# The second mixing layer's end in two token halves, with the fetching tokens' searches beside the second half

## The chip, the cores and the metric

The kernel runs as one program on one NeuronCore of a Trainium2 chip. The metric is device time in microseconds (us) of one execution; lower is better. The core has five engines that run side by side: TensorE (PE, matmuls; its weight loads are listed apart as PEld), VectorE (DVE), ScalarE (ACT), GpSimd (POOL, here almost only issuing indirect DMAs) and SyncE (SP, here issuing weight loads). Sixteen DMA engines move data between HBM and the on-chip memory (SBUF).

## The reference

Two transformer blocks over 512 tokens of width 1024, all in float32. The first block (a gated linear attention beside a latent attention, then a mixture of 64 experts) is not touched. What follows is the second block's end, cut to what matters:

```python
# mixing layer: y_a (recurrence) and y_b (convolution) are 512 wide, gates 2 x 1024
g_a, g_b = split(sigmoid(gates), 2)            # gates = h @ w_in[:, ...]
merged = g_a * (y_a @ w_branch_hg) + g_b * (y_b @ w_branch_conv)
x = x + merged @ w_out
# retrieval layer over 16384 single-neuron experts
hf = rmsnorm(x, norm_ffn_g)
q = (hf @ w_query).reshape(t, 8, 2, 128)        # 8 heads, two halves
s1, s2 = q[:, :, 0] . keys1, q[:, :, 1] . keys2 # 128 scores each
v1, i1 = top_k(s1, 16); v2, i2 = top_k(s2, 16)
top_s, top_pos = top_k(v1[:, None] + v2[None], 16)
idx = (i1 * 128 + i2)[top_pos]; gate = softmax(top_s)
act = gelu(expert_u[idx] . hf)                  # 8*16 rows per token
x = x + sum(gate * act * expert_v[idx])
out = rmsnorm(x, norm_final_g)
```

## The kernel before

The four phases are functions: `phase_a` (first mixing layer), `phase_b` (the expert layer), `phase_c` (second mixing layer), `phase_d` (retrieval layer and output). Activations are kept feature by token: `hx` is 128 partitions x 8 blocks x 512 tokens. Instructions are not written in their final order: a planner simulates the program's timeline and gives each engine a fixed queue, taking at each moment the ready instruction of the best priority, which by default is the order of writing. A tile belongs to a pool and a tag with a number of buffers; an instruction that needs a buffer waits until an earlier tile has been released, and a pool that is opened where a closed one lay waits, tile by tile, for what lay there. The retrieval layer's last loop fixes PE's order by hand (`manual_schedule`).

**Weights.** `k.load` (L1541) brings a 1 MB piece on SP's queue into a ring of 4 buffers. `phase_c` adds a second ring of 2 for its whole length, so six pieces can be there. `split` (L59 on ACT, L60 on DVE) turns a piece of weights into a high and a low part with two buffers for each; `mm3` (L71) multiplies with three matmuls per 128 rows.

**End of `phase_c`.** For eight output blocks `u`, two `unit`s (gates `ga`, `gb`: 24 matmuls each) are followed, one block behind, by two `branch`es (`wa`, `wb`: 12 matmuls each), all 512 tokens wide; then eight blocks of `w2_out` (24 matmuls) are added to `hx` (L1103), squared (L1105) and summed by a 128x32 matmul (L502). Then come the norm's factors (L1108 to L529).

**`phase_d`.** Tokens 0 to 255 (the fetching tokens) get their experts' rows by indirect DMA; tokens 256 to 511 are computed densely against all 16384 experts in 128 chunks. In order of writing:

- norm of both halves into new tiles (L1161), `hx` written to DRAM as `hdr` and freed;
- `first(h, 0)` for eight heads: query matmuls (L1198), a copy, key matmuls (L1205), and `best`: the 16 best of 128 (L1178 to L1190); `rows_of` turns the fetching tokens to rows;
- `second(0)`, `second(1)`: the 16 best of the sums, their gates and expert numbers (to L1269). After that `gathered_u` can run: 256 gathers of 128 rows of `peer_u` (L1346 on POOL, 0.5 MB each), each dotted with its tokens on DVE (L1355). Six row buffers; 206 gathers are written before the dense loop ends, the others in the last loop;
- 128 chunks `u_chunk` (L1328: 8 matmuls of 256 tokens, each as two instructions, and a Gelu). The first `JR` = 68 results stay in SBUF (`ge`), the next `JP` = 60 go to DRAM (`st`). Beside the first 68 run `first(h, 1)` and `second(2)`, `second(3)`; beside the other 60 run 64 `gates` steps, one per chunk, which build the dense gates of four tokens on DVE (L1299, L1304, L1315), ACT (L1306, L1311) and PE (L1309);
- the last loop: 64 pairs of chunks of `peer_v` (L1495), with gathered rows of `peer_v` (L1346, L1384: four per pair) and the last 50 `peer_u` gathers between them. `residual` (L1337, L1339) adds `hdr` back through one buffer `hr`. Row buffers: 6 in `sb` and 6 in `lp`.

The pool `ep` holds the tiles of searches and gates; `lp` (with `hr`, `z` and rows) is opened in its place after it closes.

Of the kernel before, what the change touches and what calls it, by code (L numbers as in the profile page):

```python
# [511 lines left out]
def group_cols(k, s, out):  # L512

    for j in range(T // 128):
        k.nc.tensor.matmul(out[:, j:j + 1], s[:, 128 * j:128 * j + 128], k.pick, start=True, stop=True)
# [18 lines left out]
def col_rows(k, p, y):  # L534

    for j in range(T // 128):
        k.nc.tensor.matmul(p[:, 128 * j:128 * j + 128], y[:, j:j + 1].to_broadcast([128, 128]), k.ident,
                           start=True, stop=True)
# [270 lines left out]
def phase_c(k):  # L809
# [5 lines left out]
    with ExitStack() as ctx:  # L815
        sb = ctx.enter_context(tc.tile_pool(name="c_sb", bufs=1, reuse_waits="tile"))
        wk = ctx.enter_context(tc.tile_pool(name="c_wk", bufs=2, reuse_waits="tile"))
        ps = ctx.enter_context(tc.tile_pool(name="c_ps", bufs=1, reuse_waits="tile", space=PS))
        k.ring2 = (ctx.enter_context(tc.tile_pool(name="c_ring", bufs=2, reuse_waits="tile")), 2)
        hg = ctx.enter_context(ExitStack())  # L820
        hp = hg.enter_context(tc.tile_pool(name="c_hg", bufs=2, reuse_waits="tile"))
# [4 lines left out]
        def tmp(name, shape=(128, T), dt=FT):  # L826
            return wk.tile(list(shape), dt, name=name, tag="t", bufs=7)
# [38 lines left out]
        lm = sb.tile([128, 1 + len(LEVELS), 64], I8, name="lm")  # L866
# [3 lines left out]
        rmask = sb.tile([128, T], FT, name="rmask")  # L870
# [15 lines left out]
        def unit(name, i):  # L886
# [8 lines left out]
            p = pm()  # L895
            mm3(k, [(p, slice(0, T))], wh, wl, xh, xl)
# [161 lines left out]
        hg.close()  # L1058


        mp = ctx.enter_context(tc.tile_pool(name="c_mp", bufs=1, reuse_waits="tile"))
        ah, al, bh, bl = (mp.tile([128, 4, T], FR, name=n) for n in ("ah", "al", "bh", "bl"))
        m = mp.tile([128, 8, T], FT, name="m")
        for y, h, l in ((ya, ah, al), (yb, bh, bl)):
            for i in range(4):
                act(h[:, i], y[:, i], AF.Copy)
                tt(l[:, i], y[:, i], h[:, i].bitcast(FT), op=OP.subtract)

        def branch(name, u, h, l):
# [4 lines left out]
            p = pm("h", 4)  # L1074
            mm3(k, [(p, slice(0, T))], wh, wl, h, l)
            return p

        gates = []
        for u in range(8 + 1):
            if u < 8:  # L1080
                gates.append([tmp("ga"), tmp("gb")])
                for t, n in zip(gates[u], ("ga", "gb")):
                    tt(t, unit(n, u), r12[:, 0], op=OP.mult)
                    act(t, t, AF.Sigmoid)
            if u >= 1:
                v = u - 1
                ga, gb = gates[v]
                tt(m[:, v], branch("wa", v, ah, al), ga, op=OP.mult)
                tt(gb, branch("wb", v, bh, bl), gb, op=OP.mult)
                tt(m[:, v], m[:, v], gb, op=OP.add)  # L1090
        mh, ml = [sb.tile([128, 8, T], FR, name=f"m{i}", tag="big", bufs=2) for i in range(2)]
        for u in range(8):
            act(mh[:, u], m[:, u], AF.Copy)
            tt(ml[:, u], m[:, u], mh[:, u].bitcast(FT), op=OP.subtract)
        sums = pm("h")
        for u in range(8):
            if u % 2 == 0:
                w = k.load(I["w2_out"][u // 2], [128, 8, 256])
            o = 128 * (u % 2)
            wh, wl = split(k, wk, w[:, :, o:o + 128], [128, 8, 128], "w8", 2)  # L1100
            p = pm()
            mm3(k, [(p, slice(0, T))], wh, wl, mh, ml)
            tt(hx[:, u], hx[:, u], p, op=OP.add)  # L1103
            sq = tmp("sq")
            act(sq, hx[:, u], AF.Square)  # L1105
            group_sums(k, sums, u, sq)
        sq = tmp("sums")
        nc.vector.tensor_copy(sq, sums)  # L1108
        pt = pm("h")
        group_cols(k, sq, pt)  # L1110
        ts(k.rcol[:, 0], pt[:, 0:4], 1.0 / D, EPS, op0=OP.mult, op1=OP.add)
        k.rstd = col_rsqrt(k, sb, k.rcol[:, 0], "rd", k.rcol[:, 1])
    k.ring2 = (None, 0)


def phase_d(k):
# [10 lines left out]
    JR, JP = 68, 60  # L1127
# [3 lines left out]
    with ExitStack() as ctx:  # L1131
        dr = ctx.enter_context(tc.tile_pool(name="d_dram", bufs=1, space=bass.MemoryType.DRAM))
        sb = ctx.enter_context(tc.tile_pool(name="d_sb", bufs=1, reuse_waits="tile"))
        pg = ctx.enter_context(tc.tile_pool(name="d_pg", bufs=2, reuse_waits="tile", space=PS))
# [16 lines left out]
        rstd = pm("g", 2)  # L1151
        col_rows(k, rstd, k.rstd)

        xs = [ep.tile([128, 4, N0], FT, name="xs", tag="kept", bufs=3) for _ in range(2)]
        x = sb.tile([128, 8, ND], FT, name="x")
        ht = [sb.tile([128, D], FT, name=f"ht{j}") for j in range(NS)]
        for s in range(2):
            o = slice(N0 * s, N0 + ND * s)
            for c in range(8):
                y = x[:, c] if s else xs[c // 4][:, c % 4]  # L1160
                stt(y, hx[:, c, o], gain("norm_ffn_g_2", c), rstd[:, o], op0=OP.mult, op1=OP.mult)  # L1161

        hdr = dr.tile([128, 8, T], FT, name="hdr")
        nc.scalar.dma_start(hdr, hx)
        k.free_h()
        keys = ep.tile([128, 2048], FT, name="keys", tag="big").rearrange("p (a b) -> p a b", a=16)
        nc.scalar.dma_start(keys, I["peer_keys"])

        def rows_of(j):
            for c4 in range(2):  # L1170
                p = pm("o", 3)
                for c in range(4):
                    nc.tensor.transpose(p[:, 128 * c:128 * c + 128], xs[c4][:, c, 128 * j:128 * j + 128], k.ident)
# [18 lines left out]
        def first(h, s):  # L1192

            w = k.load(I["peer_wq"][h], [128, 8, 256])
            for side in range(2):
                p = pm()
                for c in range(8):
                    nc.tensor.matmul(p[:, 0:256], w[:, c, 128 * side:128 * side + 128],  # L1198
                                     x[:, c] if s else xs[c // 4][:, c % 4], start=c == 0, stop=c == 7)
                q = ep.tile([128, 256], FT, name="q", bufs=3)  # L1200
                act(q, p[:, 0:256], AF.Copy)
                p = pm("o", 3)
                for j in range(2):
                    o = slice(128 * j, 128 * j + 128)
                    nc.tensor.matmul(p[:, o], q[:, o], keys[:, 2 * h + side], start=True, stop=True)  # L1205
                best(side, h, 2 * s, p)

        ia = [sb.tile([128, 128], I32, name=f"ia{j}") for j in range(NS)]
        iat = [sb.tile([128, 128], I32, name=f"iat{j}") for j in range(NS)]
        gg = [sb.tile([128, 128], FT, name=f"gg{j}") for j in range(NS)]  # L1210
# [199 lines left out]
        for h in range(8):  # L1410
            first(h, 0)
            if h < NS:
                rows_of(h)
# [258 lines left out]
```

## Time and profile before

| what | us |
|---|---|
| median of 3 runs (lowest, highest) | 3018.57 (3017.64, 3019.36) |
| the profiled execution | 3018.37 |
| its span, first to last instruction | 3016.6 |

| engine | busy us | share of the span |
|---|---|---|
| PE | 2713.6 | 90% |
| PEld | 1594.1 | 53% |
| DVE | 1224.5 | 41% |
| ACT | 623.2 | 21% |
| POOL | 591.7 | 20% |

The mean granted PE clock is 0.958 of 2.4 GHz. The DMAs moved 912.93 MB, a mean of 303 GB/s. The shares are means over stages that have different limits, so stretches of the span are read one by one: a row of a stretch gives its length, each engine's busy time with the number of its instructions, the granted clock, the mean busy share of the DMA engines and their GB/s. In a timeline a row is a run of like instructions: start, length, engine, line, operation, output and inputs, shape, count, and in brackets the idle time before it with what ended it. Durations of neighbouring instructions overlap, so the pace is read from the distance of starts.

### The profile page before, as it was taken

What the parts mean: (1) busy time and instruction counts of PE and PEld (TensorE: products, weight loads), DVE (VectorE), ACT (ScalarE), POOL (GpSimd) and SP (SyncE); (2) the same over time, 40 slices, a digit from 0 to 9 for tenths busy, and PEclk for the clock granted to TensorE, in tenths of its full rate; (3) what the DMA queues carried; (4) which work ended last, traced back from release to release, by engine and by line L of the source; (5) the groups of instructions that cost most, each with busy time, mean ns of one, the idle gap of its engine ahead of it and who ended that gap; (6) DMA issues with size and microseconds to landing.
All of it is one profiled execution on the core that took longest, in us unless ns stands there. A gap on an engine that the chain in (4) does not pass through costs nothing. (4 is left out here: it accounts for less than half of the span.)

```text
span 3016.6 us, 35266 instructions
## 1 busy us (share of the span) xinstructions
PE 2713.6 (90%) x13794; PEld 1594.1 (53%) x13794; DVE 1224.5 (41%) x3040; ACT 623.2 (21%) x1304; POOL 591.7 (20%) x600
## 2 busy tenths in 40 slices
PE   8999888887888777699999997999998499999997
PEld 6877422322232222377777786888887333333332
DVE  5444411111111111268855389985888522200001
ACT  4333200000000000265333121122555300000000
POOL 1000100000000000000000005454433256544442
PEclk9979999999999999899999998999999699999999
DMA  4104899999999999912113239999999699999996
GB/s 158 42 1 154 367 421 421 421 421 421 420 421 420 421 421 376 376 60 85 56 56 112 92 132 355 365 381 361 379 363 350 225 399 412 412 410 363 401 401 252
DMA packets 185453, 912.93 MB, mean 303 GB/s; under 512 B 18864, under 2 KB 38464, under 8 KB 112192
## 3 DMA queue, kind: packets, MB, share of 16 engines
q1 hardware_dynamic: 83664, 602.85, 49.7%
q0 software_dynamic: 73728, 268.47, 23.0%
q10 hardware_dynamic: 27888, 39.29, 3.6%
q8 instruction: 110, 1.80, 0.2%
q14 instruction: 63, 0.52, 0.0%
HBM read 890.61 MB, written 19.92 MB: 302 GB/s over the span
## 5 line engine op out<-in xcount | busy, mean ns | idle before, releaser
L1328 PE MATMUL pa<-x,w 128*128 128x256 f32 x2048 | 455.4, 381 | 0.0
L1328 PEld LDWEIGHTS pa<-x,w 128*128 128x128 f32 x2048 | 385.9, 191 | 50.6
L1355 DVE SCALAR_TENSOR_TENSOR rows<-rows,ht 128x1024 f32<-128x1024 f32 x256 | 310.5, 1218 | 237.5 <-DMA rows<-in_peer_u_rows,ia 211.4
L1346 POOL DMA_INDIRECT rows<-in_peer_u_rows,ia x256 | 287.8, 1124 | 440.1 <-DVE rows L1355 211.1
L1346 POOL DMA_INDIRECT rows<-in_peer_v,iat x256 | 253.0, 988 | 292.1 <-PE os L1384 151.1
L712 PE MATMUL pr<-w,xs 128*32 128x512 f32 x1024 | 212.4, 697 | 91.6 <-DMA w<-in_expert_up 91.4
L732 PE MATMUL px<-w,ht 128*32 128x512 f32 x1024 | 223.2, 599 | 44.9 <-DMA w<-in_expert_down 35.5
L1495 PE MATMUL o<-w,ge 128*128 128x512 f32 x544 | 243.4, 600 | 0.0
L1495 PE MATMUL o<-w,gl 128*128 128x512 f32 x480 | 215.5, 602 | 4.4 <-DVE gl L1481 4.4
L71 PE MATMUL pm<-xg,w8h 128*128 128x512 f32 x640 | 206.4, 402 | 3.5 <-ACT cc L942 1.4
L712 PE MATMUL pg<-w,xs 128*32 128x512 f32 x1024 | 178.7, 612 | 19.3 <-DMA w<-in_expert_gate 19.3
L960 POOL MEMSET acc<- 128x1024 f32 x1 | 1.0, 952 | 936.4 <-PE px L732 936.4
L712 PEld LDWEIGHTS pr<-w,xs 128*32 128x32 f32 x1024 | 46.0, 124 | 245.1 <-DMA w<-in_expert_up 168.7
L1495 PEld LDWEIGHTS o<-w,ge 128*128 128x128 f32 x544 | 100.8, 191 | 139.4 <-issue 139.4
L732 PEld LDWEIGHTS px<-w,ht 128*32 128x32 f32 x1024 | 53.4, 109 | 203.0 <-DMA w<-in_expert_down 95.8
L718 DVE SCALAR_TENSOR_TENSOR hd<-pr,ga,hd 128x512 f32<-128x512 f32 x16 | 12.0, 751 | 361.6 <-PE pr L712 361.6
L1495 PEld LDWEIGHTS o<-w,gl 128*128 128x128 f32 x480 | 89.4, 191 | 131.0 <-issue 122.9
L1384 PE MATMUL os<-rows,z 128*32 128x512 f32 x1024 | 144.6, 600 | 5.4 <-DMA rows<-in_peer_v,iat 4.3
L1481 DVE TENSOR_TENSOR gl<-gl,g 128x256 f32<-128x256 f32 x60 | 21.5, 420 | 305.2 <-DMA gl<-st 305.2
L71 PEld LDWEIGHTS pm<-xg,w8h 128*128 128x128 f32 x640 | 120.8, 190 | 33.7 <-ACT w8h L59 2.0
L745 DVE TENSOR_TENSOR hT<-hT,po 128x512 f32<-128x512 f32 x128 | 86.0, 687 | 128.7 <-PE po L744 127.3
L59 ACT ACTIVATE w8h<-w 128x1024 fp32r<-128x1024 f32 (+3 forms) x101 | 90.8, 901 | 218.7 <-PE pm L71 106.3
(561 smaller groups left out, 3601.8 us busy)
## 6 DMA issues: line engine op xcount, KB each, us to landing
w<-in_expert_up SPq DMA_DIRECT2D x128, 1024.0 KB, 19.8
w<-in_expert_gate SPq DMA_DIRECT2D x128, 1024.0 KB, 19.8
w<-in_expert_down SPq DMA_DIRECT2D x128, 1024.0 KB, 19.8
w<-in_peer_u SPq DMA_DIRECT2D x64, 1024.0 KB, 8.1
w<-in_peer_v SPq DMA_DIRECT2D x64, 1024.0 KB, 8.3
w<-in_peer_wq SPq DMA_DIRECT2D x16, 1024.0 KB, 4.8
w<-in_w_out SPq DMA_DIRECT2D x8, 1024.0 KB, 4.8
st<-kept ACTq DMA_DIRECT2D x15, 512.0 KB, 9.3
```

The lines of the kernel that those rows point to most:

```text
L59: nc.scalar.activation(hi, src, AF.Copy)
L71: nc.tensor.matmul(o, w[:, c, :], x[:, c, s], start=first and c == 0 and n == 0, stop=last and c == kc - 1 and n == 2)
L712: nc.tensor.matmul(p[s], xs[:, 4 * half + c, s], ws[e][:, c], start=half == 0 and c == 0, stop=half == 1 and c == 3, skip_group_check=True)
L718: stt(hd, pu, ga[:, 1:2], hd, op0=OP.mult, op1=OP.mult)
L732: nc.tensor.matmul(pd[n][s], ht[:, 2 * half + f, s], ws[e][:, f, 512 * n:512 * n + 512], start=half == 0 and f == 0, stop=half == 1 and f ...
L745: tt(hx[:, c], hx[:, c], p, op=OP.add)
L1328: nc.tensor.matmul(p[:, :ND], w[:, c], x[:, c], start=c == 0, stop=c == 7)
L1346: nc.gpsimd.indirect_dma_start(out=r, out_offset=None, in_=rows, in_offset=bass.IndirectOffsetOnAxis(ap=idx, axis=0))
L1355: stt(r, r, 1.0, ht[j], op0=OP.mult, op1=OP.mult, accum_out=dots[:, n:n + 1])
L1384: nc.tensor.matmul(po[i][32 * g:32 * g + 32], z[:, o:o + 32], rs[g][:, 512 * i:512 * i + 512], start=r == 0, stop=r == 31, skip_group_chec ...
L1481: tt(b, b, g[:, :, j], op=OP.mult)
L1495: nc.tensor.matmul(out[NS + t][c], w[:, 128 * t:128 * t + 128], vp[:, i % 2, 512 * c:512 * c + 512], start=i == 0, stop=i == NJ - 1, skip_ ...
```

## The change

The end of `phase_c` runs the whole chain (gates, branches, out, sums, norm factors) for tokens 0 to 255 and then again for 256 to 511, with matmuls 256 wide; each half loads and splits all weights. The second ring is closed with the recurrence's pools, so the ring has four buffers there. Halves of `hdr` are written as they are done, and the norm is made in place in `hx`, which now lives until the searches and dense chunks are done. Norm, `first`, `rows_of` and `second` of the fetching tokens are given the priority of the second half's beginning, and use the two PSUM banks "g"; scores lie in the same bank as their query. `JR` and `JP` become 64 and 64. Pools are laid out anew: `ge` at the bottom of phase C's place, then `lo` (gates' tiles, 3 row buffers; usable after the second half), `sb` (3 row buffers) and `ep` above; later `lp` with 3. Keys are loaded head by head, for each half.

```diff
@@ phase_c
+        hg = ctx.enter_context(ExitStack())
+        k.ring2 = (hg.enter_context(tc.tile_pool(name="c_ring", bufs=2, ...)), 2)
...
         hg.close()
+        k.ring2 = (None, 0)
+        HT = T // 2
+        mp = ctx.enter_context(tc.tile_pool(name="c_mp", bufs=1, reuse_waits="tile"))
+        pt6 = ctx.enter_context(tc.tile_pool(name="c_pt", bufs=1, ..., space=PS))
+        def pm(tag="m"):
+            return pt6.tile([128, 512], FT, ..., bufs={"m": 3, "h": 2, "s": 1}[tag])
...
+        for s in range(2):
+            S = slice(HT * s, HT * s + HT)
+            if s:
+                k.second_half = tc.cur_priority
+            yh, yl = (mp.tile([128, 8, HT], FR, name=f"y{i}", tag=f"y{i}") for i in range(2))
...
+                    for t, n in zip(gates[u], ("ga", "gb")):
+                        tt(t, unit(n, u, S, pm), r12[:, 0, S], op=OP.mult)
+                        act(t, t, AF.Sigmoid)
...
+            mh, ml = [mp.tile([128, 8, HT], FR, name=f"m{i}", tag=f"y{i}") for i in range(2)]
...
+                mm3(k, [(p, slice(0, HT))], wh, wl, mh, ml)
+                tt(hx[:, u, S], hx[:, u, S], p, op=OP.add)
+                sq = tmp("sq")
+                act(sq, hx[:, u, S], AF.Square)
+                group_sums(k, sums, u, sq)
+            nc.scalar.dma_start(k.hdr[:, :, S], hx[:, :, S])
...
@@ phase_d
-    JR, JP = 68, 60
+    JR, JP = 64, 64
...
+        ge = [gp.tile([128, n, ND], FT, name=f"ge{i}") for i, n in enumerate((JA, JR - JA))]
+        lo = ctx.enter_context(tc.tile_pool(name="d_lo", bufs=1, reuse_waits="tile"))
         sb = ctx.enter_context(tc.tile_pool(name="d_sb", bufs=1, reuse_waits="tile"))
...
+        x = [hx[:, :, 0:N0], hx[:, :, N0:]]
+        def norm(s):
+            rstd = pm("g", 2)
+            col_rows(k, rstd, k.rcol[:, 1, 2 * s:2 * s + 2], 2)
             for c in range(8):
+                stt(x[s][:, c], x[s][:, c], gain("norm_ffn_g_2", c), rstd[:, 0:256], ...)
...
-                p = pm()
+                p = pm() if s else pm("g", 2)
...
-                p = pm("o", 3)
+                r = p[:, 256:512]
...
-        rp.append((sb, 6))
+        rp.append((sb, 3))
+        with tc.high_priority(offset=tc.cur_priority - k.second_half):
+            norm(0)
+            for h in range(8):
+                first(h, 0)
+                if h < NS:
+                    rows_of(h)
+            for j in range(NS):
+                for _ in second(j):
+                    pass
+                pull(ga, 3)
+        norm(1)
+        rp.append((lo, 3))
...
         early.close()
+        k.free_h()
...
-        rp.append((lp, 6))
+        rp.append((lp, 3))
...
-            y = sb.tile([128, D], FT, name="rows", bufs=6)
+            y = sb.tile([128, D], FT, name="rows", bufs=3)
```

## Rows read from the trace of the kernel before

**Rows 1.** Stretches: length, busy us (instructions) of PE, PEld, DVE, ACT, POOL, clock, DMA

```profile
1500.00:1698.00 198.00, 193.09 (x802) 147.88 (x800) 90.07 (x120) 59.98 (x83) 2.16 (x2) 0.97 0.21 75
1698.00:1809.00 111.00, 107.78 (x528) 94.73 (x529) 83.47 (x464) 25.28 (x41) 0.00 (x0) 0.97 0.41 143
1809.00:1831.00 22.00, 1.40 (x8) 0.92 (x7) 18.70 (x38) 1.29 (x3) 16.60 (x13) 0.64 0.84 312
1831.00:2097.00 266.00, 265.95 (x1258) 234.33 (x1258) 217.80 (x701) 47.98 (x106) 131.86 (x116) 0.99 0.97 376
2097.00:2328.00 231.00, 230.26 (x1348) 200.77 (x1345) 194.50 (x440) 128.15 (x403) 85.11 (x74) 1.00 0.94 356
2328.00:2401.00 73.00, 23.50 (x150) 18.89 (x150) 48.45 (x116) 30.41 (x95) 24.09 (x19) 0.56 0.71 240
2401.00:2680.00 279.00, 274.11 (x914) 99.08 (x914) 59.52 (x97) 0.71 (x2) 161.09 (x159) 1.00 1.01 401
2680.00:2982.00 302.00, 301.31 (x1097) 114.85 (x1095) 17.21 (x48) 1.67 (x4) 125.64 (x133) 1.00 1.02 393
```

**Rows 2.** Timeline of PE, end of the first idle stretch

```profile
1830.45 0.47 PE L1269 MATMUL po<-cst,nn 128*128 128x128 f32 x1 [20.60 <-DVE nn L1267]
```

**Rows 3.** Timeline of PE, from the last dense chunk to the last loop

```profile
2324.74 1.94 PE L1495 MATMUL o<-w,ge 128*128 128x512 f32 x4
...
2385.31 3.62 PE L1339 MATMUL o<-cst,hr 128*128 128x128 f32 x16 [10.71 <-DMA hr<-hdr]
...
2397.12 3.78 PE L1339 MATMUL o<-cst,hr 128*128 128x128 f32 x16 [6.47 <-DMA hr<-hdr]
2400.69 4.39 PE L1495 MATMUL o<-w,ge 128*128 128x512 f32 x8
```

**Rows 4.** Stretch of the gates steps, columns as in rows 1

```profile
2097.00:2376.00 279.00, 244.53 (x1460) 211.74 (x1457) 238.93 (x545) 158.55 (x497) 104.53 (x89) 0.92 0.88 328
```

**Rows 5.** Timeline of PE, 512 columns wide, and the sums between two blocks

```profile
1660.34 0.40 PE L71 MATMUL pm<-m,w8l 128*128 128x512 f32 x1
...
1661.04 0.40 PE L71 MATMUL pm<-m,w8l 128*128 128x512 f32 x1
...
1662.54 1.04 PE L502 MATMUL ph<-sq,cst 128*32 128x512 f32 x2
1663.52 0.51 PE L71 MATMUL pm<-m,w8l 128*128 128x512 f32 x1
```

**Rows 6.** Timeline of PE in phase A: the same three matmuls, 264 columns

```profile
25.65 0.65 PE L71 MATMUL uu<-xg,w8h 128*128 128x264 f32 x4
...
26.38 0.64 PE L71 MATMUL uu<-xg,w8h 128*128 128x264 f32 x4
```

**Rows 7.** Groups by line: busy us, mean ns, idle us before and releasers

```profile
L60 DVE TENSOR_TENSOR w8l<-w,w8h 128x1024 fp32r<-128x1024 f32 x71 | 87.6, 1235 | 35.6 <-ACT w8h L59 34.9
L59 ACT ACTIVATE w8h<-w 128x1024 fp32r<-128x1024 f32 x71 | 74.9, 1056 | 140.1 <-PE pm L71 52.7 <-PE uu L71 23.4 <-issue 17.8
L1355 DVE SCALAR_TENSOR_TENSOR rows<-rows,ht 128x1024 f32<-128x1024 f32 x256 | 310.5, 1218 | 237.5 <-DMA rows<-in_peer_u_rows,ia 211.4 <-issue 16.9 <-PE o L1495 7.7
```

**Rows 8.** DMA issues: count, size, median us from issue to landing

```profile
w<-in_w_ga SPq DMA_DIRECT2D x4, 1024.0 KB, 4.8
```

**Rows 9.** Timeline of DVE: last addition, norm, two searches, first sums

```profile
1696.87 0.69 DVE L1103 TENSOR_TENSOR hT<-hT,pm 128x512 f32<-128x512 f32 x1 [4.93 <-PE pm L71]
...
1704.83 3.22 DVE L1161 SCALAR_TENSOR_TENSOR xs<-hT,vecs,pg 128x256 f32<-128x256 f32 x8 [2.23 <-PE pg L537]
...
1771.77 0.30 DVE L1178 MAX8 tv<-po 128x8 f32<-128x128 f32 x1 [0.95 <-PE po L1205]
...
1775.67 0.30 DVE L1178 MAX8 tv<-po 128x8 f32<-128x128 f32 x1 [0.94 <-PE po L1205]
...
1776.75 0.54 DVE L1221 TENSOR_TENSOR cand<-tv,tv 128x384 f32<-128x384 f32 x1
```

**Rows 10.** Timeline of POOL: the first gather

```profile
1809.27 1.16 POOL L1346 DMA_INDIRECT rows<-in_peer_u_rows,ia  x1 [124.51 <-DVE sm L1234]
```

More of the change, by code (lines that the diff above doesn't have):

```diff
@@ L509, in col_sums, with group_cols @@
             k.nc.tensor.matmul(out[:, j:j + 1], x[:, t0:t0 + 128], k.ones[:, 0:1], start=c == 0, stop=c == len(xs) - 1)
-def group_cols(k, s, out):
-    for j in range(T // 128):
+def group_cols(k, s, out, n=T // 128):
+    for j in range(n):
         k.nc.tensor.matmul(out[:, j:j + 1], s[:, 128 * j:128 * j + 128], k.pick, start=True, stop=True)
@@ L531, in col_rsqrt, with col_rows @@
     return out
-def col_rows(k, p, y):
-    for j in range(T // 128):
+def col_rows(k, p, y, n=T // 128):
+    for j in range(n):
         k.nc.tensor.matmul(p[:, 128 * j:128 * j + 128], y[:, j:j + 1].to_broadcast([128, 128]), k.ident,
@@ L1058, in phase_c, with tmp @@
         hg.close()
+        k.ring2 = (None, 0)
+        HT = T // 2
         mp = ctx.enter_context(tc.tile_pool(name="c_mp", bufs=1, reuse_waits="tile"))
[L1062 to L1067, printed above, removed]
+        pt6 = ctx.enter_context(tc.tile_pool(name="c_pt", bufs=1, reuse_waits="tile", space=PS))
+        def pm(tag="m"):
+            return pt6.tile([128, 512], FT, name="p" + tag, tag=tag, bufs={"m": 3, "h": 2, "s": 1}[tag])
+        def tmp(name):
+            return mp.tile([128, HT], FT, name=name, tag="t", bufs=6)
         def branch(name, u, h, l):
@@ L1091, in phase_c @@
[L1091 to L1106, printed above, removed]
@@ L1194, in first @@
             w = k.load(I["peer_wq"][h], [128, 8, 256])
+            keys = ep.tile([128, 2, 128], FT, name="keys", bufs=2)
+            nc.scalar.dma_start(keys, I["peer_keys"][:, 2 * h:2 * h + 2])
             for side in range(2):
[L1196 removed]
+                p = pm() if s else pm("g", 2)
                 for c in range(8):
[L1198 to L1200 removed]
+                    nc.tensor.matmul(p[:, 0:256], w[:, c, 128 * side:128 * side + 128], x[s][:, c],
+                                     start=c == 0, stop=c == 7)
+                q = ep.tile([128, 256], FT, name="q", bufs=2)
                 act(q, p[:, 0:256], AF.Copy)
[L1202 removed]
+                r = p[:, 256:512]
                 for j in range(2):
                     o = slice(128 * j, 128 * j + 128)
[L1205 to L1210, printed above, removed]
[L1211 to L1212 removed]
+                    nc.tensor.matmul(r[:, o], q[:, o], keys[:, side], start=True, stop=True)
+                best(side, h, 2 * s, r)
+        hk = lo.tile([128, 2, ND], F16, name="hk")
+        hg = lo.tile([128, 2, ND], FT, name="hg")
         def second(j):
@@ L1296, in gates @@
                     p = pm("g", 2)
-                    o1, o2, oh, ol = (ep.tile(sh, F16, name=f"o{n}", bufs=2) for n in range(4))
+                    o1, o2, oh, ol = (lo.tile(sh, F16, name=f"o{n}", bufs=2) for n in range(4))
                     for n, o in enumerate((o1, o2)):
@@ L1327, in u_chunk @@
             for c in range(8):
-                nc.tensor.matmul(p[:, :ND], w[:, c], x[:, c], start=c == 0, stop=c == 7)
+                nc.tensor.matmul(p[:, :ND], w[:, c], x[1][:, c], start=c == 0, stop=c == 7)
             act(dst, p[:, :ND], AF.Gelu)
@@ L1408, in routing @@
                 yield from second(j)
[L1410 to L1413, printed above, removed]
-        rp.append((sb, 6))
-        gp = ctx.enter_context(tc.tile_pool(name="d_ge", bufs=1, reuse_waits="tile", side="right"))
-        ge = [gp.tile([128, n, ND], FT, name=f"ge{i}") for i, n in enumerate((JA, JR - JA))]
-        rt, ga = routing(), chain(*(gathered_u(j) for j in range(NS)))
-        for j in range(NS):
-            for _ in second(j):
-                pass
-            pull(ga, 3)
-        taken = [0]
-        def some(n):
-            taken[0] += n
-            pull(ga, n)
+        rt, ga = routing(), chain(*(gathered_u(j) for j in range(NS)))
+        rp.append((sb, 3))
[11 more added lines that the diff above has]
+        rp.append((lo, 3))
         st = dr.tile([128, JP, ND], FT, name="st")
@@ L1558, in body @@
     nc.gpsimd.memset(k.eps, EPS)
+    k.dr = ctx.enter_context(tc.tile_pool(name="dram", bufs=1, space=bass.MemoryType.DRAM))
+    k.hdr = k.dr.tile([128, 8, T], FT, name="hdr")
     phase_a(k)
```

111 lines of the change are left out of this document (58 added, 53 removed).

## The prediction

> **What bounds the kernel now.** The stretches come first, because no engine bounds the whole span. From 1500 to 1698 (the end of the second mixing layer) PE is busy 193 of 198 us, DVE 90, ACT 60, and the DMA engines a fifth [rows 1]: matmuls bound it. From 1698 to 1809 (norm, queries and searches of the fetching tokens) PE is again the bound. Then PE stands still for 20.60 us, waiting for DVE's expert numbers [rows 2], and only at 1809.27 is the first gather issued [rows 10]. From 1831 to 2097 PE, DVE and DMA are all nearly full (266, 218 us, share 0.97); from 2097 to 2376 (gates steps) DVE is busy 239 of 279 and PE 245 [rows 4]. PE has done its last dense chunk by 2324.74, but 14 of 64 gates steps are still to do (of the 150 PE instructions after 2328, some 112 are theirs, eight to a step), so it mostly idles until 2400.69, at a mean clock of 0.56; the last steps end at 2376, then it waits 10.71 and 6.47 us for the residual `hr` [rows 1, 3]. From 2401 on the last loop runs with PE full and DMA share 1.01 to 1.02: two limits at once. So the program can only become shorter ahead of 2401: 20.6 us at 1809 and about 70 us at 2328, and what the change costs must be taken from these.
>
> **Term 1, half-width products.** The 768 matmuls of 512 columns become 1536 of 256. Three of 512 take 0.70 us, 0.233 each [rows 5]; six of 264 take 0.73, 0.122 each, with as many weight loads [rows 6]. At 256 I take 0.119: 1536 x 0.119 - 768 x 0.233 = +4 us (0 at half of 0.233, +8 at 0.122). The sums after each output block come 16 times instead of 8, half as wide; one costs 0.98 us now [rows 5]: +2 (0 to +8).
> A rule of the Trainium skill (TensorE: Matmul & The Clock Gate, "The mechanism" and "LDWEIGHTS") speaks against this: a weight load takes its number of columns over 1.2 GHz and overlaps a running matmul only in another row group. By it 768 more loads of 128 columns are an estimated 82 us.
> The trace disagrees: in the rows of 264 columns a load and a matmul together take 0.122 us, about what 264 columns take at 2.4 GHz. I go by the rows.
>
> **Term 2, splits.** Each half splits all weights again: 24 wide splits at 1.06 us on ACT and 1.23 on DVE [rows 7] and 16 half as wide, some 40 us more of DVE, plus some 10 for 64 operations cut in two. DVE and ACT have room for it (108 and 138 us idle in that stretch). But the split parts have two buffers: the split of a gate block waits for the product two before it, and hides behind one branch, now 12 x 0.119 = 1.4 us, where it needs 2.3. In the first half nothing else is there for PE: 8 x 1 us, and 2 more where the merged halves lie in the place of `y`. +10 (0 to 8 x 2.3 = +18). In the second half the searches' matmuls fill this.
>
> **Term 3, weights again.** 16 more pieces of 1 MB come while the DMA engines are at a share of 0.21 [rows 1]: hidden, 0; were they not, 16.8 MB at the 400 GB/s of the last loop would be 42 us. But the ring has four buffers there, not six. Two hold `wa` and `wb` for four blocks, two turn over `ga` and `gb`. In the first half a new piece lands in 4.8 us [rows 8] against 60 x 0.119 = 7.1 us of matmuls: hidden. In the second half eight pieces of queries want the same buffers. A load that nothing hides costs 4.8 and the split 2.3. Of 24 loads I take between one and two as open: +10 (0 to eight open: +57).
>
> **Term 4, the stall at 1809.** Searches run beside the second half; whatever DVE does late, PE has other work. -20.6 [rows 2]; the smaller end is 0, if the same wait comes back before the second half's norm.
>
> **Term 5, when the gathers begin.** The second half begins near 1500 + 99 + 13 (half of term 1, and term 2) = 1612. From the last addition to the norm are 8.0 us, the norm takes 3.2 [rows 9]: 1623. In it `hx` is overwritten, so the write of this half of `hdr` must have landed; it starts with the same 8 us, so I take 0 (to +8). Alone, a search takes 3.9 us [rows 9], 16 of them 62; beside the second half (70 us of DVE's own) I take 5.5, 88 us: 1711. From the first sums to the first gather are 32.5 us [rows 9, 10]; I take 40: **1751** instead of 1809 (1717 if DVE were free, 1805 if all waits for the second half). PE's own work is the second half (99 + 3 + 10) and some 70 us of the moved searches (from their part of 1698 to 1809): to 1794, with the norm 1805. Until then only `sb`'s three row buffers can be used: some 20 gathers. From 1831 to 2097 there were 116 in 266 us, 2.3 us each [rows 1]; I keep that pace, as that stretch is full in DVE and DMA.
>
> **Term 6, the gates steps.** The dense chunks would end on PE at 2324.7 + 16 + 10 - 20.6 = 2330, and with 14 more gates steps among them (some 0.45 us each) at 2336. The steps begin after chunk 64, not 68: four chunks of 16 instructions of some 0.22 us are 14 us, so 2097 + 5 - 14 = 2088. By then 20 + 283 / 2.3 = 143 gathers are out; 129 (13 + 116) were by 2097, and some 214 (129 + 85) when the steps ended. In the old stretch DVE did some 85 dot products at 1.22 us [rows 7], 104 of its 239 us; the other 135 are some 62 steps, 2.2 each. New: 64 x 2.2 + 71 x 1.22 = 228 us. At the old busy share of 86% [rows 4] that ends at 2354, with PE as the pace at 2336; I take 2350: **-26** against 2376.
>
> **Term 7, into the last loop.** 24.7 us pass from 2376 to the loop [rows 3]. `hr` then lies where the searches' tiles were, and no longer under tiles of the gates steps, which moved to `lo`; the first load can come before the steps end, and the second right after the first is used. Between 0 (if ACT's queue keeps the load behind the steps) and -20 I take **-12**.
>
> **Term 8, the last loop.** Nine row buffers, not twelve. DMA is full there, so what is missing is three rows fetched ahead, 3 x 0.52 MB at 401 GB/s: +4. If rows then came too late in each pair it would be more, but a gather has a whole pair of time behind it even with nine. Four more chunks come back from DRAM (1 MB, beside a PE that is full: +1; if open, +3). The last output tile waits for one of three buffers: +1. Together +6 (0 to +9).
>
> **Sum.** The profiled execution took 3018.37 us, 1.8 above its span and 0.2 below the median of the three runs. -26 - 12 + 6 = -32: 2986 us. About 0.2% (6 us) is what a measurement of this kernel tells from no change.
>
> **The rivals.**
> - All is hidden. Searches fill every gap and the ring is enough: terms 1 to 3 cost 4 instead of 26, PE ends its chunks and steps at 2314, the steps two after the last, near 2318 (-58), `hr` gives 20, the loop loses 2: -76, **2942**. For it: 108 us of idle DVE before 1698. Against: the first half has no other work for PE, and DVE's 228 us would have to fit into some 248.
> - The gathers start no earlier. Expert numbers and gates of the fetching tokens lie near the foot of `sb`, where by the sizes written the second half's temporaries end; if they wait for these, the first gather comes at 1805. Then 123 are out at 2088, 91 dot products and 64 steps are 252 us, at 86% until 2381: +5 - 12 + 6 = -1, **3017**. For it: a pool opened in an old place waits tile by tile. Against: the numbers lie last of the four, just at the edge.
> - Slower: the ring starves in the second half. `wa` and `wb` sit on two of four buffers, queries on a third, and PE meets an open load at every second block: eight loads of 7.1 us, +57 in place of +10. All later terms move with it: +15, **3033**. From five or six open loads on the change loses. For it: the six pieces held now are used without a gap over 6 us in all (193 of 198), which says nothing of four. Against: a waiting mixing block leaves PE to a query block, and the reverse.
> - Slower still: weight loads do not hide at half width. PEld was busy 147.88 us for 800 loads, 0.185 each [rows 1]; 768 of them open are 142 us: **3128**. Against it stand [rows 6], where this is measured. The rule of the Trainium skill quoted in term 1 (TensorE: Matmul & The Clock Gate) would make it so.
>
> **How the numbers follow.** Forecast 0.54 (its own range 2968 to 3002); all hidden 0.16; gathers no earlier 0.12, of which two fifths are faster, a third within 6 us and the rest slower; ring 0.14; weight loads 0.02; 0.02 for something unseen, slower. Faster by over 0.2%: 0.52 + 0.16 + 0.05 = 0.73. Within 0.2%: 0.06. Slower: 0.14 + 0.02 + 0.02 + 0.03 = 0.21. The range is 2946 to 3036: it takes in most of "all hidden", all of the forecast with its bounds, and the starving ring; what is left out is the best corner (0.06) and the weight loads with the worst of the ring (0.08).
>
> **What would show it.** In the profile after: a pace near 0.119 us for the 256-wide products (term 1); PE gaps of about 1 us ahead of the first half's gate blocks (2); waits of PE or of splits for `w_ga`, `w_wa` or `peer_wq` in the second half (3); no 20 us gap at the second index transpose (4); a first gather near 1751, and some 20 before the dense chunks begin (5); the last gates step near 2350 with few steps after PE's last chunk (6); the last loop beginning 5 to 15 us after it (7); and 610 to 622 us from there to the end (8). The prediction is wrong if the first gather is not ahead of 1790, if the second half with its searches takes PE more than 30 us above 180, or if the last loop, its rows now nearer to their use, grows by over 15 us.

## The result, and the profile after

| | us |
|---|---|
| before, median of 4 runs (lowest, highest) | 3018.11 (3009.39, 3019.36) |
| after, median of 4 runs (lowest, highest) | 3102.53 (3099.86, 3117.73) |
| ratio, 95% interval | 1.0296 (1.0258 to 1.0335) |
| forecast (range) | 2986 (2946 to 3036) |

The changed kernel is slower by 84 us; its time lies outside my range, and beyond the rival of a starving ring (3033). Its profiled execution took 3099.86 us, its span 3098.1. First the stretches after, columns as in [rows 1]:

```profile
1507.90:1630.00 122.10, 109.22 (x833) 102.16 (x832) 76.57 (x123) 54.34 (x94) 0.00 (x0) 0.95 0.42 149
1630.00:1742.50 112.50, 103.36 (x798) 96.26 (x796) 67.14 (x143) 47.58 (x77) 0.00 (x0) 1.00 0.46 163
1742.50:1876.00 133.50, 63.55 (x297) 53.58 (x297) 91.68 (x459) 18.98 (x28) 19.46 (x15) 0.76 0.35 118
1876.00:2419.80 543.80, 535.77 (x2790) 469.88 (x2789) 429.45 (x1174) 182.36 (x524) 236.83 (x199) 0.99 0.95 359
2419.80:2465.40 45.60, 22.39 (x140) 17.02 (x138) 29.51 (x79) 26.63 (x86) 6.34 (x4) 0.62 0.57 185
2465.40:3098.10 632.70, 600.47 (x2076) 222.60 (x2074) 87.50 (x173) 9.34 (x26) 297.53 (x295) 0.99 0.97 373
```

Three places lose. The halves end at 1742, not 1698. Then PE idles 70 of 133.5 us, where before it idled 3 us up to 1809 and 20.6 up to 1831 [rows 1, 2]. And the last loop takes 632.7 us, where it took 615.9 (2400.69 to 3016.6, [rows 3]). Only the way into the loop is shorter. (The rows are the two token halves, the searches, the dense chunks with the gates steps, the way into the loop, and the loop.)

The searches did not move. SP's timeline (start, time over which the issues reach, count) shows the eight query pieces behind every piece of the second half:

```profile
1652.39 0.33 SPq L1551 DMA_DIRECT2D w<-in_w_ga  x1
1690.10 10.42 SPq L1551 DMA_DIRECT2D w<-in_w_out  x4
1704.27 69.35 SPq L1551 DMA_DIRECT2D w<-in_peer_wq  x8
```

Head 0 is then searched inside the half, but head 1 only after it. PE has transposed the fetching tokens by 1726.5, and ACT copies the result only once the half is over:

```profile
1722.86 0.60 PE L1188 MATMUL pg<-cst,hT 128*128 128x128 f32 x4
1725.84 0.66 PE L1188 MATMUL pg<-cst,hT 128*128 128x128 f32 x4
...
1742.53 7.15 PE L1215 MATMUL pg<-hT,w 128*128 128x256 f32 x32
```

```profile
1740.46 0.55 ACTq L1123 DMA_DIRECT2D hdr<-hT  x1
1741.06 1.08 ACT L1189 ACTIVATE ht<-pg 128x512 f32<-128x512 f32 x2 [0.18 <-issue]
```

Until then both banks "g" (two of PSUM's, where PE leaves its results) are held, and the next query (1742.53) needs one. And the dense chunks, PE's filler in this place before, stand behind the last transpose of expert numbers:

```profile
1849.78 0.48 PE L1283 MATMUL pg<-cst,nn 128*128 128x128 f32 x1 [35.85 <-DVE nn L1281]
1872.53 0.47 PE L1283 MATMUL pg<-cst,nn 128*128 128x128 f32 x1 [22.27 <-DVE nn L1281]
1872.80 1.06 PE L537 MATMUL pg<-cst,rcol 128*128 128x128 f32 x4
1875.50 1.22 PE L1342 MATMUL pa<-hT,w 128*128 128x256 f32 x2 [1.64 <-DVE hT L1182]
```

L537 is the norm of the dense half. It takes a bank "g" too, and is written after `second(1)`, so the first chunk (L1342) comes at 1875.50. The first gather, on POOL:

```profile
1852.13 1.37 POOL L1360 DMA_INDIRECT rows<-in_peer_u_rows,ia  x1 [354.94 <-DVE gg L1279]
```

### The profile page after: what moved, and what is told of

Same layout as the page of the kernel before. It is cut to its first block, busy times and chain, and to the rows that moved or that the text cites. A ratio compares the mean times of both kernels' runs of the same rounds, so it can differ in the third digit from the quotient of the medians.

```text
span 3098.1 us, 37210 instructions
## 1 busy us (share of the span) xinstructions
PE 2730.3 (88%) x14578; PEld 1636.6 (53%) x14578; DVE 1271.6 (41%) x3155; ACT 660.8 (21%) x1384; POOL 607.5 (20%) x600
## 4 chain that ended last, share of the span: by engine, by line
PE 40%; issue 6%; DVE 5%; DMA 5%; POOL 4%; ACT 2%; SPq 0%; DVEq 0%; POOLq 0%; ACTq 0%
PE pa L1342 14%; PE o L1505 8%; PE pm L71 7%; POOL rows L1360 4%; PE os L1398 2%; PE pg L1215 2%; PE pa L1215 2%; DMA gl<-st 2%; DMA w<-in_expert_up 1%; DVE w8l L60 1%; PE pg L1323 1%; PE pm L911 1%; PE ph L71 1%; DMA rows<-in_peer_v,iat 1%; ACT w8h L59 1%
## 5 line engine op out<-in xcount | busy, mean ns | idle before, releaser
L1342 PE MATMUL pa<-hT,w 128*128 128x256 f32 x2048 | 457.8, 381 | 1.8 <-DVE hT L1182 1.6
L1360 POOL DMA_INDIRECT rows<-in_peer_u_rows,ia x256 | 313.8, 1226 | 699.1 <-DVE gg L1279 354.9
L1342 PEld LDWEIGHTS pa<-hT,w 128*128 128x128 f32 x2048 | 384.9, 190 | 52.9 <-DVE hT L1182 1.9
L1505 PE MATMUL o<-w,gl 128*128 128x512 f32 x512 | 231.1, 605 | 10.4 <-DVE gl L1491 10.4
L1505 PE MATMUL o<-w,ge 128*128 128x512 f32 x512 | 230.4, 602 | 0.0
L71 PE MATMUL pm<-xg,w8h 128*128 128x256 f32 (+1 forms) x896 | 218.6, 335 | 8.2 <-ACT w8h L59 6.2
L59 ACT ACTIVATE w8h<-w 128x1024 fp32r<-128x1024 f32 (+4 forms) x141 | 126.1, 896 | 220.5 <-PE pm L71 98.4
L71 PEld LDWEIGHTS pm<-xg,w8h 128*128 128x128 f32 x896 | 152.3, 191 | 27.3 <-ACT w8h L59 7.1
L60 DVE TENSOR_TENSOR w8l<-w,w8h 128x1024 fp32r<-128x1024 f32 (+4 forms) x141 | 144.7, 1028 | 52.4 <-ACT w8h L59 50.1
L71 PE MATMUL pm<-xg,w8l 128*128 128x256 f32 (+1 forms) x448 | 150.5, 337 | 10.1 <-DVE w8l L60 10.1
```

The source lines that it names most:

```text
L59: nc.scalar.activation(hi, src, AF.Copy)
L60: nc.vector.tensor_tensor(lo, src, hi.bitcast(FT), op=OP.subtract)
L71: nc.tensor.matmul(o, w[:, c, :], x[:, c, s], start=first and c == 0 and n == 0, stop=last and c == kc - 1 and n == 2)
L1342: nc.tensor.matmul(p[:, :ND], w[:, c], x[1][:, c], start=c == 0, stop=c == 7)
L1360: nc.gpsimd.indirect_dma_start(out=r, out_offset=None, in_=rows, in_offset=bass.IndirectOffsetOnAxis(ap=idx, axis=0))
L1505: nc.tensor.matmul(out[NS + t][c], w[:, 128 * t:128 * t + 128], vp[:, i % 2, 512 * c:512 * c + 512], start=i == 0, stop=i == NJ - 1, skip_ ...
```

## The experiments

The runs were measured in three groups, each beside runs of the kernel before; the medians of that kernel were 3015.7 (e1 to e4), 3016.1 (e5 to e8) and 3016.5 (e9 to e11). A ratio is to the kernel before of the same group.

**e1_norm_bank.**

```diff
-            rstd = pm("g", 2)
+            rstd = pm() if s else pm("g", 2)
```

> The changed kernel with one edit: the norm of the dense half takes its PSUM bank from the three banks of the chunks, not from the two banks g. Theory A (the banks g are handed out in the order of writing, so this norm and all dense chunks stand behind the last transpose of expert numbers): chunks fill PE's 70 us of idle time between 1742 and 1876; PE idles less than 25 us there, the last dense chunk ends some 45 us earlier (2419 to about 2375). The first gather stays near 1852, so the gates steps end where they did plus or minus 10 and a part comes back as a tail: 3075 to 3085 in all. Rival (the chunks would wait anyway, for peer_u pieces behind the query pieces in the ring): within 5 us of 3102.

Measured: 3082.62 us, ratio 1.0229 (1.0212 to 1.0246). The same stretch as in the third row above:

```profile
1742.50:1876.00 133.50, 96.89 (x469) 83.08 (x468) 85.49 (x486) 24.42 (x39) 3.75 (x3) 0.88 0.29 100
```

PE is busy 96.9 us where it was 63.6, and the last dense chunk ends at 2377 (2419). Theory A holds for the greater part: with another bank the chunks come, so the order of banks kept them away. But the rival holds for the first of it. The norm has its bank and is done on DVE by 1758.4; the first chunk comes only after the eight query pieces, once SP has issued the first piece of `peer_u` at 1790.39:

```profile
1796.60 2.75 PE L1342 MATMUL pa<-hT,w 128*128 128x256 f32 x12
```

36.6 us stay idle (I said under 25), 25.3 of them in one wait for DVE, and the first gather slips to 1871.64, since chunks now stand between the searches. Of the 42 us by which the last chunk ends earlier, 20 come back in time.

**e2_shift.**

```diff
-        rp.append((sb, 3))
+        rp.append((sb, 2))
-        rp.append((lo, 3))
+        rp.append((lo, 4))
...
```

(A third changed line gives the rows of the last loop four buffers in `lo`, where they had three in `sb`.)

> The changed kernel with the pool of gathered tokens, gates and expert numbers moved 4 KB up (one row buffer goes from it to the pool below), so that it no longer lies over the last 3.5 KB of the mixing layer's temporaries. Theory B (the whole pool waits for those temporaries, so the copies of the transposed tokens wait for the end of the second half and hold both banks g from 1726 to 1741): head 1 is searched from about 1727 on and not from 1742, the first gather comes 10 to 15 us earlier than 1852 and the time falls by 10 to 15 us, to about 3088. Rival (tiles wait one by one and these do not overlap anything): no change, 3102. By both, head 0 is not searched before 1715, as its weights still come behind the second half's in the ring.

Measured: 3127.25 us, 1.0370 (1.0339 to 1.0400), 25 us slower than the changed kernel. The mechanism of theory B came out: the copies no longer wait for the half's end,

```profile
1724.34 0.60 ACT L1189 ACTIVATE ht<-pg 128x512 f32<-128x512 f32 x1 [0.25 <-PE pg L1188]
1727.38 0.60 ACT L1189 ACTIVATE ht<-pg 128x512 f32<-128x512 f32 x1
```

but its price did not: the first gather comes at 1846.65, 5.5 us earlier and not 10 to 15. By the sizes written, the mixing layer's temporaries (`c_mp`) reach some 3.5 KB into the pool `sb`, whose first 4 KB hold `dots`, `gg`, `iat` and `ia`; `ht`, into which these copies go, lies behind them and over no temporary. Yet its copies waited: here the pool waited as a whole, and not tile by tile, as I had written of pools. The edit hurt elsewhere: the last loop took 641 us, and the last chunk ended at 2452. Why is asked in e5.

**e3_wq_own.** Query pieces of the fetching tokens in two buffers of their own:

```diff
-            w = k.load(I["peer_wq"][h], [128, 8, 256])
+            if s:
+                w = k.load(I["peer_wq"][h], [128, 8, 256])
+            else:
+                w = wqp.tile([128, 8, 256], FT, name="wq")
+                nc.sync.dma_start(w, I["peer_wq"][h])
```

> The changed kernel with the query weights of the fetching tokens in two buffers of their own (in the place of tiles that only the later sums need), not in the ring of four. Theory C (the ring gives its buffers in the order of writing, so these eight pieces come after all 12 pieces of the second half, at 1704): the first search is done near 1650 and not 1723. If theory B of the pool that lies over the temporaries holds too, the banks g are then held to the end of the second half and heads 1 to 7 stay behind 1742: first gather about 1843 (one head, 9.9 us, less), 3090. If only the ring held them back, all 16 searches run beside the second half: first gather before 1800, under 3050.

Measured: 3099.68 us, 1.0281 (1.0255 to 1.0306). Head 0 is searched by 1661.98, the first search of head 1 is done only at 1760, as by theories C and B together: two locks in a row. The gain I expected from one head (12 us) did not show: the first gather came at 1855.82, 3.7 us later than in the changed kernel. Why stays open. ACT's copies again, in this kernel:

```profile
1746.40 0.55 ACTq L1123 DMA_DIRECT2D hdr<-hT  x1
1746.99 1.08 ACT L1197 ACTIVATE ht<-pg 128x512 f32<-128x512 f32 x2 [0.18 <-issue]
```

**e4_all.** The edits of e1, e2 and e3.

> All three edits together. If A, B and C are the whole reason why the searches did not move, this does what the change was meant to do: the 16 searches run between 1640 and 1760 beside the second half, PE has the second half and the searches done near 1805, the chunks follow without a pause, first gather near 1785, last chunk near 2345, last loop from about 2365, then 632 us as in the changed kernel: 2990 to 3005. Rival (the halves and the searches together starve in the split weights, DVE or the ring): PE done with both not before 1840, then 3035 or more.

Measured: 3117.92 us, 1.0338 (1.0316 to 1.0360): far above the forecast. The number is the rival's, its reason is not: the second half's last addition ends at 1808.6, before the 1840 that the rival asked for. All 16 searches are done by 1765 and the first gather comes at 1814.69, so the three locks were what kept the searches in their old place; but the last chunk ended at 2399.7, and the loop took 684 us.

**e5_all_slots.** e4_all, with the row buffers taken one by one:

```diff
-        rp.append((sb, 2))
+        rp[:] = [(sb, 2)] * 2
-        rp.append((lo, 4))
+        rp[:] = [(sb, 2)] * 2 + [(lo, 4)] * 4
-        rp.append((lp, 3))
+        rp += [(lp, 3)] * 3
```

> As e4_all, but gathers take the row buffers one by one in a fixed round (2 and 4, later 2, 4 and 3), not a pool at each turn. With pools in turn the pool of two is used every second (later every third) time, so e4_all and e2_shift had in effect four buffers ahead of the last loop and six in it, against six and nine in the changed kernel. Theory D (that, and not the searches' new place, is what made e4_all slow: its searches did run beside the second half, first gather 1815): six gathers again in flight, last chunk near 2365 (2400 in e4_all), last loop 620 to 635 us (684): 3000 to 3020. Rival (the second half with the searches beside it is slow by itself, DVE being full from 1750 to 1850): last chunk still near 2395, only the loop becomes shorter: 3055 or more.

Measured: 3047.37 us, 1.0107 (1.0082 to 1.0132), 70 us under e4_all: theory D holds for the difference, the size I gave (3000 to 3020) does not. Here the change does what it was meant to do: the second half's last addition ends at 1796.6, the searches before it. End of the last search, first gather, and the stretch between:

```profile
1752.61 0.17 DVE L1213 CAST ti<-ix 128x32 f16<-128x32 uint32 x1
```

```profile
1802.70 2.09 POOL L1373 DMA_INDIRECT rows<-in_peer_u_rows,ia  x1 [74.57 <-DVE rd1y L524]
```

```profile
1750.00:1800.00 50.00, 40.45 (x260) 34.96 (x258) 47.72 (x196) 23.39 (x35) 0.00 (x0) 0.90 0.43 150
```

DVE is busy 47.7 of 50 us with splits and sums: it bounds the move. The first gather is 6.6 us earlier than before [rows 10], no more. The last chunk ends at 2352.9, even before the 2365 of theory D, and the loop takes 633.8 us, as it said. What it left out lies between them: the gates steps (DVE busy 235 of 280 us) go on to 2390 (2374 before), and the loop begins at 2405.8. In this trace that is 5 us after the 2400.7 before, and the loop is 18 us longer.

**e6_before_nine.** The kernel before with nine row buffers in its last loop:

```diff
-        rp.append((sb, 6))
+        rp += [(sb, 6)] * 6
-        rp.append((lp, 6))
+        rp += [(lp, 3)] * 3
```

> The kernel before with three row buffers fewer in the last loop (nine, taken one by one), nothing else. Theory E (the last loop is limited by the DMA engines as much as by PE, and a row has a pair of time behind it even with nine): 3016 to 3024, the term 8 of the prediction. Rival (nine buffers make the rows late and are the reason for the changed kernel's 632 us instead of 616): 3030 to 3035.

Measured: 3031.47 us (10 runs), 1.0050 (1.0032 to 1.0068): the rival. The last stretches of [rows 1], in this kernel, and what POOL's gathers waited for from 2401 to 2982 (us, times, longest):

```profile
2401.00:2680.00 279.00, 272.18 (x888) 97.38 (x886) 59.47 (x97) 0.71 (x2) 148.68 (x156) 1.00 1.00 396
2680.00:2982.00 302.00, 291.16 (x1042) 111.41 (x1041) 17.18 (x48) 1.59 (x3) 120.32 (x128) 0.98 0.99 374
```

```profile
POOL rows L1346 <- PE os L1384: 240.3, 55, 21.1
POOL rows L1346 <- DMA rows<-in_peer_v,iat: 1.8, 6, 0.3
```

The same two rows in the kernel before:

```profile
POOL rows L1346 <- PE os L1384: 158.8, 58, 7.4
POOL rows L1346 <- DMA rows<-in_peer_v,iat: 57.3, 43, 2.5
```

With twelve buffers a gather often waits only for the gather ahead of it to land, with nine almost always for PE to give a row back. So the DMA engines move less (from 2680 to 2982 a share of 0.99 for 1.02, 374 GB/s for 393), and PE idles 10.8 of these 302 us where it idled 0.7. The loop takes 632.2 us, as good as the changed kernel's 632.7.

**e7_no_move.**

```diff
-        with tc.high_priority(offset=tc.cur_priority - k.second_half):
+        if True:
             norm(0)
+            norm(1)
...
-        norm(1)
```

(and query and norm take chunk banks.)

> The changed kernel without the move: norm of both halves, searches and sums of the fetching tokens come after the second half in their old priority, with the chunks' PSUM banks; halves, ring of four and the new layout stay. It prices the halves alone. Theory F (the halves cost what the traces show: 234 us for 192, less the 9.5 us of one search that ran inside them, about 33 us, and the last loop 6 to 17): the second half ends near 1732, first gather near 1842, 3055 to 3068. Rival (the halves are nearly free as I predicted, terms 1 to 3, and the 80 us come from the move alone): under 3045.

Measured: 3063.96 us, 1.0156 (1.0128 to 1.0184): theory F. From the recurrence's last products (PE) to the last addition (DVE) it takes 232.9 us,

```profile
1503.28 0.69 PE L1036 MATMUL ph<-acc,v 128*64 128x128 f32 x4 [0.81 <-DVE acc L1014]
```

```profile
1736.19 0.42 DVE L1118 TENSOR_TENSOR hT<-hT,pm 128x256 f32<-128x256 f32 x1 [3.19 <-PE pm L71]
```

and before 191.4, from this row to the last addition at 1696.87 [rows 9]:

```profile
1505.48 0.69 PE L1035 MATMUL ph<-acc,v 128*64 128x128 f32 x4 [0.81 <-DVE acc L1013]
```

The halves alone cost 41.5 us. In this trace the loop begins 33 us later than before and is 10.5 us longer. The kernel as changed is some 39 us slower than this one without the move (medians of two groups).

**e8_before_turn.** The kernel before, with the two transposes that PE stood still for written later:

```diff
-                nc.tensor.transpose(p[:, 0:128], n, k.ident)
-                act(iat[j], p[:, 0:128], AF.Copy)
...
+                if n in (24, 28):
+                    turned(n // 4 - 6)
```

> The kernel before with one edit: the two transposes of expert numbers (needed only by the later gathers) are written among the dense chunks, at chunks 24 and 28, so that PE's queue does not stop at them. Theory G (the 20.6 us at 1809 are only the order of PE's queue): no idle time of PE there, the last chunk ends 20 us earlier (2307); the gates steps start earlier too but DVE paces them, so of the 20 us between 5 and 15 stay: 3003 to 3012. Rival (chunks cannot run there either, as DVE and the query pieces are late): within 3 us of the kernel before.

Measured: 3006.35 us (10 runs), 0.9963 (0.9949 to 0.9977): as by theory G. From 1800 to 1850 PE is busy 48.1 of 50 us:

```profile
1800.00:1850.00 50.00, 48.13 (x230) 41.70 (x229) 48.36 (x181) 11.25 (x18) 21.91 (x19) 1.00 0.83 327
```

The last chunk ends 15 us earlier (the row after it: 2309.41 for 2324.74, [rows 3]); about 10 us stay.

**e9_late_residual.** e8 with the residual later in the loop:

```diff
-                    if i == 0:
+                    if i == 8 + 8 * t:
                         residual(out[NS + t], NS + t)
```

> e8_before_turn with the residual added later in the last loop (at its steps 8 and 16 for the dense tokens, at the twelfth pair of each gathered half instead of at the first), so that nothing waits for hr at the loop's start. Theory H (the 10.3 and 6.2 us of waiting for hr stand on the path): PE starts the loop's matmuls about 14 us earlier; the loop then shares the DMA engines with the first gathers, so 8 to 14 us stay: 2992 to 2998. Rival (the loop is paced by the DMA engines, which worked through those waits): within 3 us of e8_before_turn, 3006.

Measured: 3004.93 us, 0.9957 (0.9941 to 0.9974): the rival; the 1.4 us under e8 are not clear of noise. Nothing waits for `hr` any more; the loop's matmuls begin at 2374.7 and it ends no earlier. Those waits cost next to nothing, as the DMA engines go on through them. In the kernel before, from the last gates step to the loop's eight matmuls, PE is busy 8.9 of 26.1 us and the DMA share is 0.99:

```profile
2374.60:2400.70 26.10, 8.93 (x38) 7.62 (x38) 4.77 (x12) 0.57 (x1) 5.63 (x6) 0.63 0.99 320
```

**e10_three_splits.** e7 with three buffers for each split part, which also moves them from the pool `wk` into the halves' own:

```diff
+        wk, WB = mp, 3
...
-            wh, wl = split(k, wk, w[:, :, o:o + 128], [128, 8, 128], "w8", 2)
+            wh, wl = split(k, wk, w[:, :, o:o + 128], [128, 8, 128], "w8", WB)
```

> e7_no_move (halves, no move of the searches) with three buffers for each split part of the weights in the halves, not two. Theory I (the split of a gate block waits for the product two before it, at half width 1.4 us, so each output block loses 0.85 us of PE): a gate-and-branch block takes 8.6 to 8.7 us instead of 9.42, the second half ends 12 to 14 us earlier (1736 to about 1723), 3050 to 3054 in all. Rival (DVE's chain of product, gate and split in one queue sets the 9.42 us, whatever the buffers): the block stays above 9.2 us and the time at 3064.

Measured: 3055.00 us, 1.0127 (1.0106 to 1.0147). One output block of gates and branches takes 16.72 us in the kernel before, 9.42 at half width in the changed one, and 8.57 here (five blocks between its two rows). The rows are DVE's product at the same place of a block: kernel before, changed kernel, this one.

```profile
1594.44 0.69 DVE L1083 TENSOR_TENSOR ga<-pm,r 128x512 f32<-128x512 f32 x1 [3.06 <-PE pm L71]
1611.16 0.69 DVE L1083 TENSOR_TENSOR ga<-pm,r 128x512 f32<-128x512 f32 x1 [3.06 <-PE pm L71]
```

```profile
1674.16 0.42 DVE L1098 TENSOR_TENSOR ga<-pm,r 128x256 f32<-128x256 f32 x1 [1.13 <-PE pm L71]
1683.58 0.42 DVE L1098 TENSOR_TENSOR ga<-pm,r 128x256 f32<-128x256 f32 x1 [1.13 <-PE pm L71]
```

```profile
1544.97 0.43 DVE L1100 TENSOR_TENSOR ga<-pm,r 128x256 f32<-128x256 f32 x1 [0.71 <-PE pm L71]
...
1587.80 0.42 DVE L1100 TENSOR_TENSOR ga<-pm,r 128x256 f32<-128x256 f32 x1 [0.69 <-PE pm L71]
```

Theory I holds for the block. Of 13 us 5.5 are left at the end of the halves (1730.7), as PE now stands 11.8 us at the start, waiting for ACT's first split (e7: 4.9). By the layout that split now lies over tiles of the recurrence, and the pool waits longer for them; this was not tested apart.

**e11_half.** e9 with `JR, JP = 64, 64`.

> e9_late_residual with 64 results kept on chip and 64 sent to DRAM (68 and 60 before), the one part of the change's new numbers that the prediction booked as a gain (term 6: the gates steps begin four chunks earlier). If that holds, the gates steps end some 5 us earlier for 1 MB more of traffic: 2 to 6 us under e9_late_residual. Rival (DVE paces the steps and the gathers alike, and the four chunks come back in the last loop): the same within 3 us, or slower.

Measured: 2993.24 us, 0.9929 (0.9910 to 0.9947), 12 us under e9, more than I gave it; the two intervals just touch. The steps' weight loads begin at 2058.7 (2081.9 in e9) and end at 2343.3 (2373.6); 9 us of that are an earlier first gather in this run (1805.04 for 1813.82). It is the fastest version, and the only part of the change in it is this one line.

## Why the prediction was wrong

Two steps failed. The first is the one on which terms 4 and 5 rest: "Searches run beside the second half; whatever DVE does late, PE has other work." They did not, so the first gather came at 1852 and not at 1751, and PE stood still for 58.1 us where the sum had taken 20.6 away. I took the priority of the searches for their place in time. A priority orders instructions that are ready; these lacked a buffer. The ring gave its buffers in the order of writing (query pieces at 1704, e3), so did the banks "g" (first chunk at 1875, e1), and the pool that lies partly over an older one waited for it as a whole (copies at 1741, e2). I named the last as a rival, for the expert numbers alone and "just at the edge"; the ring I read backwards, as starving PE.

The second step is the prices. With the three locks gone (e5) the searches do run beside the second half, and the time is still 3047, 61 us over the forecast. The halves cost 41.5 us and not 26, the last loop 15 to 18 and not 6, and DVE, which I took to have room beside the second half, holds the first gather to 1803. Two of the signs that I gave for its being wrong came true: the first gather is not ahead of 1790, and the loop grew by 16.8 us.

- **Term 1** (+6): right. Three matmuls of 256 take 0.355 us in the first half (0.118 each), and the sums after an output block, two instructions, 0.55 by their starts. Each of these matmuls has a weight load of its own in the same rows, and none of it shows in that pace. So the trace speaks against the rule of the Trainium skill (TensorE: Matmul & The Clock Gate, "The mechanism" and "LDWEIGHTS"), an estimated 82 us by its figure.
- **Term 2** (+10): the mechanism right, the size within its own bounds. A pause of 0.85 us per block comes in both halves, 14 us, as no search filled the second (in e5 they do: PE is busy 118.75 of 120 us from 1630 to 1750). e10 shows the two buffers as its cause.
- **Not in the sum**: before, the first gate product (24 matmuls) is multiplied during the recurrence's last, thin steps. After, it is not; by the layout the halves' pools lie in the recurrence's place and wait for it. PE pauses three times there (4.67, 1.40 and 1.76 us) and runs on at the lower of its clock's two levels, 1.2 GHz: three matmuls of 256 take 0.64 us near 1510, and 0.355 from 1513 on. Then it pauses 4.94 us for a split (below), which stands on ACT behind a split of `y` that has itself waited 7.30 us for DVE:

```profile
1489.75 2.05 PE L1012 MATMUL ph<-qx,kx 128*128 128x128 f32 x8 [4.67 <-DVE qx L1008]
...
1521.05 0.80 PE L71 MATMUL pm<-xg,w8h 128*128 128x256 f32 x2 [4.94 <-ACT w8h L59]
```

  Of the 41.5 us, an estimated 17 are the slower blocks (16 x 1.07: 9.44 in e7 for half of 16.72 before) and 3 the output blocks (16 x 0.21), by the pace of some of them; the other 21 lie at the starts of the two halves. That these are this fill alone was not separated.
- **Term 3** (+10): PE never waits for a weight piece in the halves. The ring of four cost by its order, not by its depth.
- **Term 4** (-20.6): the two waits for a transpose of expert numbers are 58.1 us together, where there was one of 20.6 [rows 2]. e8 shows that the 20.6 were PE's queue at a transpose that nothing needed yet. In the changed kernel the chunks stood behind the norm's bank: e1 fills 33 of the 70 idle us. Writing its transposes later was not tried.
- **Term 5** (1751): 1852, and 1803 where the searches do run beside the half. I gave a search 5.5 us and 40 to the sums, but let DVE's splits and the sums of two token blocks pass beside them; DVE is full there (47.7 of 50 us in e5).
- **Term 6** (-26): not there, as the gathers came late. In e5, where they do not, the steps still take 280 us (2110 to 2390), not the 262 that I summed. The part that needs no move, 64 and 64, is real: 12 us in e11.
- **Term 7** (-12): right. From the last gates step (2449.4) to the loop's eight matmuls (2465.44) are 16.0 us, 10 fewer than before (26.1: the last gates step there ends at 2374.6, not at the round 2376 of the sum). By e9 such a wait is worth next to nothing where the DMA engines go on.
- **Term 8** (+6): 16.8, and e6 shows 15 for the buffers alone. "A gather has a whole pair of time behind it even with nine" was wrong: with nine, gathers waited 240 us in all for PE to give a row back, where it was 159.

As an account: 41.5 (halves) + 15 (nine buffers) - 12 (64 and 64) = 45 of the 48 us that e7 loses, and 39 for a move that didn't move and put the chunks behind it. These are prices from four kernels, and that they add was not shown. Done as meant the move is worth 17 (e7 to e5), so even then the change loses. The wait of 20.6 us, one of its two targets, was had by writing two transposes later (e8), of which 10 us came back in time.

## What to carry to other kernels

Before giving work a better priority, list each buffer that it takes (ring, PSUM bank, pool place) and who was written ahead for the same one: it moves up only to the first that is shared. Where an engine stands at one wait, ask first whether that instruction must stand there; moving it was cheaper here than filling the gap (e8 against e5). Pools used in turn are as deep as the smallest times their number (e4 to e5: 70 us), and a loop that fills both PE and the DMA engines can pay for buffers taken from it (three of twelve: 15 us).

## What the runs showed of the hardware

In the recurrence's tail eight matmuls of 128 columns take 2.05 us after, once PE had paused 4.67 us, and 1.13 before, after a pause of 3.17:

```profile
1503.54 1.13 PE L1011 MATMUL ph<-qx,kx 128*128 128x128 f32 x8 [3.17 <-DVE qx L1007]
```

The mean granted clock from 1480 to 1507 is 0.65 after and 0.96 before: for much of it the level of 1.2 GHz instead of 2.4. Three such groups lose 2.8 us on top of the pauses between them.

One weight load for each matmul of 256 columns costs no time that shows: the two together take 0.118 us.
